# Computing layer 1's memory keys during the routing of layer 0, with own buffers for expert rows

## The chip, the cores and the metric

The kernel runs on one core of a Trainium2 chip. TensorE (PE) multiplies matrices, VectorE (DVE), ScalarE (ACT) and GpSimd (POOL) do the rest, and SyncE (SP) issues most transfers (DMAs) between HBM and the on-chip memory SBUF; matmul results land in banks of PSUM. Each engine works through its own list of instructions in order and waits on semaphores for the others. The metric is the time of one execution on the device, in microseconds (us).

## What the kernel computes

A trunk of two layers on 256 tokens of width 1024, float32. Each layer adds three things to the running state h: a token mixer (layer 0: a recurrent and a sparse-attention group; layer 1: a short gated convolution), a cross-attention over 256 memory tokens, and a mixture of 16 experts. Only the last two matter here:

```python
def memory_cross_attn(xn, mem, g_mem, wq, wk, wv, wo):
    mn = rms_norm(mem, g_mem)
    q, k, v = heads(xn @ wq), heads(mn @ wk), heads(mn @ wv)     # 4 heads of 256
    p = softmax(q @ k^T * 256 ** -0.5)
    return (p @ v) @ wo

def hier_moe(xn, ...):
    # the best of 4 groups, then the best 2 of its 4 experts, gate weights from both
    for e in range(16):
        h = silu(xn @ w_gate[e]) * (xn @ w_up[e])                # 1024 -> 512
        y = y + gate[:, e:e + 1] * (h @ w_down[e])               # 512 -> 1024

for layer in range(2):
    h = h + mixer(rms_norm(h, norm_mix[layer]))
    h = h + memory_cross_attn(rms_norm(h, norm_xattn[layer]), mem, norm_mem[layer], ...)
    h = h + hier_moe(rms_norm(h, norm_ffn[layer]), ...)
return rms_norm(h, norm_final)
```

`mem` is an input, the same for both layers. The keys and values of layer 1 depend on it, on `norm_mem[1]` and on weights, and on nothing that layer 0 computes.

## The kernel before

**Matmuls.** A float32 product is made of three matmuls over a high and a low part: hi·hi, hi·lo, lo·hi. Weights come in tiles w of 1 MB (pool wpool, six buffers), and each 128x1024 piece is split into hi (ACT, L274) and lo (DVE, L275) in the pool spl (three buffers of each). Projections that give the transposed result go into a bank named FA (`proj_F`, L316, L319, L321: 128x256), the others into TA (`proj_T`, L295 to L297: 128x512). `norm_T` normalises, transposes on PE (nB, nC) and splits the result into two tiles such as m1h and m1l, of the pool act8 (four buffers b8).

**Memory keys and values.** `gen_kv(l)` (L357) is a generator of nine steps: the norm of the memory, four steps of keys (FA, into KT), four of values (TA, into VM). For layer 1 one step runs in the odd mixer, four in front of the cross-attention's queries and four between queries and scores. A scheduler of the tile framework orders the instructions of each engine; `with first()` raises the priority of what is inside, so that routing, the softmax and the first gather are pulled forward and the matmuls around them fill the gaps.

**Cross-attention** (L385). Four units of scores sB (L408), softmax on DVE and ACT (L417 to L428), transposes tC and copies to PT (L434, L435), then oB and oC (L443) and the output projection.

**Experts** (`moe`, L775). Routing makes from h: xs, h in two float16 parts (L796 to L805); posm, the place of each token in its experts' 64 seats; vals, the gates with the token numbers. Then come eight pairs of experts. `dispatch` (L554) makes the mask Pm (L561, DVE), gathers the pair's tokens with Pm and xs into banks gB (L578), and copies them with the gain into XgT (L586 ACT, L588 DVE); ptC (L597) fetches gates and row numbers. `expert_pair` (L699) runs gate and up (egA, euA, L712), the activation hs (L722 to L724), its transpose hC and hT (L729, L731), and the down product (eyA, eyO, L736). Six of a layer's pairs scale the result to rows y and scatter them to DRAM (yd<-y, L742 to L745); `add_rows` fetches them back before the last pair (yr<-yd) and adds them to h (L831); the last two pairs go back through poB (L759, L760). Pm, PG, hs, hT, y, yh and yl share the three buffers of the tag s2.

**Weights of the experts.** `Stream` (L664) loads 98 chunks per layer, 1 MB each but for a few of 0.5, in order through SP's queue into a ring of 21 slots, made of free buffers of several pools; a chunk's load is issued when the one that held its slot is used up. Where the number of chunks leaves a rest, the last ones go to the last slots of the ring.

**The overflow branch.** A group with more than 64 tokens for an expert needs extra rounds: `overflow()` reads a count into a register and branches (L812 to L821). With this input it isn't taken. It stands at BREAK = 4, between the fourth and the fifth pair; instructions can't be moved across it.

```python
if n == BREAK:
    run(cur)
    overflow()
    cur = next(pairs)
    run(cur, 3)
    continue
```

Of the kernel before, what the change touches and what calls it, by code (L numbers as in the profile page):

```python
# [9 lines left out]
F32 = mybir.dt.float32  # L10
# [18 lines left out]
NX = 7  # L29
# [30 lines left out]
def hybrid_trunk_kernel(ctx: ExitStack, tc: tile.TileContext, x, mem, positions, norm_mix, norm_xattn,  # L60
# [142 lines left out]
    def sumsq(src, engs="SV"):  # L203
        ss = sm.tile([128, 2, TT], F32, name="ss")
        for tt in range(TT):
            for half in range(2):
                square_sum(src[:, tt, half * 512:(half + 1) * 512], ss[:, half, tt:tt + 1], engs[half])
        return ss
# [26 lines left out]
    def norm_T(src, ss, g, name, xs, tags="BC"):  # L235

        rs = rstd_of(ss)
        V.tensor_scalar(xs[0], src[:, 0, :], rs[:, 0:1], None, op0=ALU.mult)
        S.activation(xs[1], src[:, 1, :], AF.Copy, scale=rs[:, 1:2])
# [13 lines left out]
        return hi, lo  # L253
# [103 lines left out]
    def gen_kv(l):  # L357

        m = kvp.tile([128, 2048], F32, tag="VM", name=f"mem{l}").rearrange("p (t d) -> p t d", t=TT)
        for tt in range(TT):  # L360
            nc.sync.dma_start(m[:, tt, :], mem[0, tt * 128:(tt + 1) * 128, :])
        mh, ml = norm_T(m, sumsq(m, "SS" if l else "SV"), gains["mem", l], f"m{l}", halves(m), tags="BC" if l else "A")
        yield
        KT = kvp.tile([128, J, T], F32, tag="KT", name="KT")
        for half in range(2):
            def use(i, b):
                S.copy(KT[:, half * 4 + 2 * i:half * 4 + 2 * i + 2, :], b)
            yield from gen_F(xa_wk[l], half * 512, 512, mh, ml, use)
        VM = kvp.tile([128, TT, D], F32, tag="VM", name="VM")
        kv_tiles[l] = KT, VM  # L370
        for half in range(2):
            def use(tt, b):
                S.copy(VM[:, tt, half * 512:(half + 1) * 512], b)
            yield from gen_T(col_loads(xa_wv[l], half * 512), mh, ml, use)

# [9 lines left out]
    def cross_attn(l, kv, n_before, n_mid):  # L385
# [9 lines left out]
        KT, VM = kv_tiles[l]  # L395
        Pt = x8([128, TT, 4, T], "Pt")
# [157 lines left out]
    def dispatch(mp, l, xs, gate, vals, posm, e0, n, by_rows):  # L554
# [12 lines left out]
        Xg = [mp.tile([128, J, 128], F32, name="XgT", tag="XgT", bufs=2) for _ in range(n // 2)]  # L567
# [24 lines left out]
        def rest():  # L592
            for pi in range(n // 2):
                if by_rows:
# [9 lines left out]
                    gsl = sm.tile([128, 1], F32, name="gslr", bufs=3)  # L604
                    V.tensor_reduce(gsl, v2[:, 0, 0:3], axis=AX.X, op=ALU.add)
                    row = sm.tile([128, 1], I32, name="row", bufs=3)
# [77 lines left out]
    class Direct:  # L684
# [5 lines left out]
        def take(self, n):  # L690
            t = self.pool.tile([128, n, 1, 512], F32, tag="XgT", name="wov", bufs=2)
            for i in range(n):
                G.dma_start(t[:, i], next(self.chunks)[1])
            return [[t[:, i, 0, :]] for i in range(n)]
# [4 lines left out]
    def expert_pair(mp, l, stream, pair, step, cuts, by_rows, ss=None, rest=None):  # L699
# [39 lines left out]
        def back_by_rows(nh):  # L739
            y = mp.tile([128, 512], F32, name="y", tag="s2", bufs=3)  # L740
# [34 lines left out]
    def moe(l, ring, fill=None, n_fill=0):  # L775
        with ExitStack() as mctx:
            mp = mctx.enter_context(tc.tile_pool(name=f"moe{l}", bufs=1, reuse_waits="tile"))
            if fill is not None:
                run(fill, n_fill)
            stream = Stream(chunks_ahead(l), ring)  # L780
            with first():
# [9 lines left out]

                xsb = act8.tile([128, 2, TT, D], F16, tag="b8", name="xs")
# [437 lines left out]
    def odd_mixer(kv, n_before):  # L1230
# [8 lines left out]
        for half in range(2):  # L1239
# [44 lines left out]
    odd_mixer(kv1, 1)  # L1284
    cross_attn(1, kv1, 4, 4)
    moe(1, ring)
# [41 lines left out]
```

## Time and profile before

| | |
|---|---|
| three runs | 993.76 us median (991.2 to 995.42) |
| the profiled execution | 989.36 us, of which the span is 987.6 |
| even mixer of layer 0 | 0 to about 193 us |
| cross-attention 0, first FA of the queries to the last TA | 193 to 266 |
| routing 0, to the first egA | 266 to 280 |
| experts 0 | 280 to 510 |
| odd mixer, cross-attention 1 | 510 to 722 |
| routing 1, experts 1 | 722 to 978 |
| busy: PE, DVE, ACT, POOL | 91%, 40%, 33%, 9% of the span |
| mean granted clock of PE | 0.96 of full speed |
| moved by DMA | 285.43 MB, mean 289 GB/s |

How to read it: a row of the list in time order has the start and the length in us, the engine, the line of the program, the operation with its tiles (out<-in) and shapes, how many of the kind follow each other, and in brackets how long the engine had been idle before, and what ended that. A matmul's length holds its whole way through the array; matmuls that follow each other overlap, so the distance of two starts is what one costs.

### The profile page before, as it was taken

To read this page: it belongs to the slowest core of one execution; us is meant where nothing else is said; L and a number is where in the kernel's file an instruction comes from. 1 tells how busy PE (TensorE), PEld (TensorE's weight loads), DVE (VectorE), ACT (ScalarE), POOL (GpSimd) and SP (SyncE) were. 2 spreads that over 40 slices of the span, in tenths; PEclk is the share of its full clock that TensorE was granted. 3 is DMA by queue.
4 is the path that set the end of the run, shared out by engine and by line. 5 is a ranking of instruction groups with operands and counts; after the bars stand their busy time and mean duration, and the time that the engine had idled before them with its cause. 6 is when DMAs were issued, how large, how long until landed. Compare 5 with 4: busy or idle time off the path is not lost.

```text
span 987.6 us, 13265 instructions
## 1 busy us (share of the span) xinstructions
PE 898.5 (91%) x5197; PEld 588.7 (60%) x5197; DVE 394.2 (40%) x830; ACT 326.2 (33%) x605; POOL 85.5 (9%) x144
## 2 busy tenths in 40 slices
PE   7999999999989995995989999999989997779795
PEld 5897588898754432332339998998855332323231
DVE  6857686635431111111337665535441111111142
ACT  5655574645411110110146445535421111111112
POOL 1000160000020000012000000000020001000201
PEclk9999899999999997998999999999999999798898
DMA  8955166577879999999875556578869999997861
GB/s 258 307 180 94 43 214 189 178 263 288 343 297 424 418 420 413 421 419 416 308 253 172 171 174 200 155 282 322 317 214 383 418 420 420 415 421 313 331 247 42
DMA packets 83022, 285.43 MB, mean 289 GB/s; under 512 B 15112, under 2 KB 16224, under 8 KB 62468
## 3 DMA queue, kind: packets, MB, share of 16 engines
q1 hardware_dynamic: 78468, 272.82, 73.3%
q0 software_dynamic: 4480, 11.65, 3.4%
q8 instruction: 44, 0.72, 0.3%
q14 instruction: 30, 0.25, 0.1%
HBM read 275.94 MB, written 11.53 MB: 291 GB/s over the span
## 4 chain that ended last, share of the span: by engine, by line
PE 35%; issue 12%; DMA 6%; DVE 2%; ACT 1%; POOL 1%; ACTq 0%; POOLq 0%; DVEq 0%
DMA yd<-y,row 6%; PE egA L712 4%; PE FA L316 4%; PE FA L319 4%; PE FA L321 4%; PE euA L712 3%; PE TA L295 2%; PE TA L296 2%; PE TA L297 2%; PE eyO L736 2%; PE eyA L736 2%; PE gB L578 2%; PE sB L408 1%; PE poB L760 0%; PE hC L729 0%
## 5 line engine op out<-in xcount | busy, mean ns | idle before, releaser
L275 DVE TENSOR_TENSOR lo<-w,hi 128x1024 fp32r<-128x1024 f32 x122 | 147.7, 1222 | 122.9 <-ACT hi L274 83.1
L274 ACT CAST hi<-w 128x1024 fp32r<-128x1024 f32 x122 | 125.9, 1047 | 86.4 <-PE FA L321 47.9
L712 PE MATMUL egA<-we,XgT 128*64 128x512 f32 x512 | 123.2, 613 | 9.9 <-issue 9.9
L712 PE MATMUL euA<-we,XgT 128*64 128x512 f32 x512 | 124.3, 600 | 0.0
L712 PEld LDWEIGHTS euA<-we,XgT 128*64 128x64 f32 x512 | 41.8, 139 | 68.9 <-issue 64.1
L712 PEld LDWEIGHTS egA<-we,XgT 128*64 128x64 f32 x512 | 38.0, 141 | 72.0 <-issue 63.8
L586 ACT ACTIVATE XgT<-gB,ffn 128x128 f32<-128x128 f32 x64 | 22.6, 367 | 175.8 <-DVE XgT L588 175.8
L578 PE MATMUL gB<-Pm,xs 128*128 128x128 f16 x512 | 41.9, 248 | 41.2 <-DVE Pm L561 41.2
L736 PE MATMUL eyA<-we,hT 128*64 128x512 f32 x256 | 73.8, 594 | 2.9 <-ACT hT L731 2.9
L736 PE MATMUL eyO<-we,hT 128*64 128x512 f32 x256 | 76.2, 593 | 0.0
L319 PE MATMUL FA<-xh,hi 128*128 128x256 f32 x272 | 71.0, 294 | 1.8 <-ACT xh L250 1.7
L578 PEld LDWEIGHTS <-xs 128*128 128x128 f16 x512 | 40.2, 151 | 54.4 <-issue 54.3
L321 PE MATMUL FA<-xl,hi 128*128 128x256 f32 x272 | 70.5, 292 | 1.8 <-DVE xl L251 1.8
L742 DVE TENSOR_SCALAR y<-eyO,gslr 128x512 f32<-128x512 f32 x12 | 9.0, 750 | 153.3 <-PE eyO L736 153.3
L319 PEld LDWEIGHTS FA<-xh,hi 128*128 128x128 f32 x272 | 53.6, 197 | 4.8 <-ACT xh L250 2.4
L321 PEld LDWEIGHTS FA<-xl,hi 128*128 128x128 f32 x272 | 53.8, 198 | 3.3 <-DVE xl L251 2.7
L745 POOL DMA_INDIRECT yd<-y,row x24 | 23.8, 991 | 283.5 <-ACT y L744 265.9
L744 ACT ACTIVATE y<-eyA,gslr 128x512 f32<-128x512 f32 x12 | 8.2, 687 | 109.4 <-PE eyA L736 97.2
L736 PEld LDWEIGHTS eyA<-we,hT 128*64 128x64 f32 x256 | 21.3, 137 | 37.8 <-issue 33.0
L736 PEld LDWEIGHTS eyO<-we,hT 128*64 128x64 f32 x256 | 21.9, 137 | 36.7 <-issue 35.0
L316 PE MATMUL FA<-xh,lo 128*128 128x256 f32 x272 | 41.7, 285 | 0.0
L229 POOL TENSOR_TENSOR rs<-ms,mhalf 128x2 f32<-128x2 f32 x9 | 6.5, 720 | 373.7 <-DVE ms L227 252.4
(419 smaller groups left out, 1546.4 us busy)
## 6 DMA issues: line engine op xcount, KB each, us to landing
we<-in_moe_w_gate_dram SPq DMA_DIRECT2D x56, 1024.0 KB, 14.2
we<-in_moe_w_up_dram SPq DMA_DIRECT2D x56, 1024.0 KB, 15.0
we<-in_moe_w_down_dram SPq DMA_DIRECT2D x52, 1024.0 KB, 13.1
w<-in_odd_w_in_dram SPq DMA_DIRECT2D x12, 1024.0 KB, 5.3
w<-in_even_w_in_dram SPq DMA_DIRECT2D x9, 1024.0 KB, 8.8
we<-in_moe_w_down_dram SPq DMA_DIRECT2D x18, 512.0 KB, 16.4
w<-in_xa_wk_dram SPq DMA_DIRECT2D x8, 1024.0 KB, 5.7
w<-in_xa_wv_dram SPq DMA_DIRECT2D x8, 1024.0 KB, 5.7
```

Source lines behind the costliest of these rows:

```text
L274: S.copy(hi, t)
L275: V.tensor_sub(lo, t, hi.bitcast(F32))
L295: P.matmul(ps[tt], xh[:, k, sl], hi, start=(k == 0), stop=False)
L296: P.matmul(ps[tt], xh[:, k, sl], lo, start=False, stop=False)
L316: P.matmul(o, lo[:, fs], xh[:, k, :], start=False, stop=(k == J - 1), skip_group_check=True)
L319: P.matmul(o, hi[:, fs], xh[:, k, :], start=(k == 0 and f % 2 == 0), stop=False, skip_group_check=True)
L321: P.matmul(o, hi[:, fs], xl[:, k, :], start=False, stop=False, skip_group_check=True)
L578: P.matmul(ps[:, jj, :], part[:, tt, :, j0 + jj], Pm[:, tt].rearrange("p e s -> p (e s)"), start=(i == 0), stop=(i == 3))
L586: S.activation(Xg[pi][:, j, :], src, AF.Copy, scale=g)
L712: P.matmul(acc[nm][i * 64:(i + 1) * 64, :], XgT[:, j, i * 64:(i + 1) * 64], ws[i][jj], start=(j == 0), stop=(j == J - 1))
L736: P.matmul(py[nh][i * 64:(i + 1) * 64, :], hT[:, j, i * 64:(i + 1) * 64], w, start=(j == 0), stop=(j == 3))
L745: G.indirect_dma_start(out=Yd[l][nh], out_offset=bass.IndirectOffsetOnAxis(ap=PT[:, 0:1], axis=0), in_=y, in_offset=None, bounds_check=2 * ...
```

## The change

Four edits. (1) The keys of layer 1 become a generator of their own, `gen_keys`: its first step, the norm of the memory, runs in the cross-attention of layer 0 after the values, with the memory in split buffers hi and lo; its four steps of keys run at the start of `moe(0)`. Layer 1 normalises the memory again and computes only values, in two steps before and two between. KT is occupied during layer 0's experts, and the pool extra has six buffers for seven (NX), so the ring has 19 slots in layer 0 and 20 in layer 1. (2) The rows y get a tag of their own with two buffers; the overflow's loads use it too, and its dispatch has its own XgT, gsl and row. (3) The dispatch of the fifth pair is called before the fourth runs on and the branch comes. (4) xs is allocated before `Stream`.

```diff
-NX = 7
+NX = 6
...
-    def gen_kv(l):
-
-        m = kvp.tile([128, 2048], F32, tag="VM", name=f"mem{l}").rearrange("p (t d) -> p t d", t=TT)
+    def mem_T(l, m):
         for tt in range(TT):
-            nc.sync.dma_start(m[:, tt, :], mem[0, tt * 128:(tt + 1) * 128, :])
-        mh, ml = norm_T(m, sumsq(m, "SS" if l else "SV"), gains["mem", l], f"m{l}", halves(m), tags="BC" if l else "A")
-        yield
+            nc.sync.dma_start(m[tt], mem[0, tt * 128:(tt + 1) * 128, :])
+        return norm_T(m, sumsq(m, "SS" if l else "SV"), gains["mem", l], f"m{l}", m, tags="BC" if l else "A")
...
+    def gen_keys(l):
+
+        mh, ml = mem_T(l, [spl.tile([128, D], F32, name="mem1", tag=t) for t in ("hi", "lo")])
+        yield
+        yield from keys(l, mh, ml)
+
+    def gen_values(l):
+
+        mh, ml = mem_T(l, in_VM(l))
+        yield
+        yield from values(l, mh, ml)
...
         run(kv, n_mid)
         KT, VM = kv_tiles[l]
+        if ahead is not None:
+            run(ahead, 1)
...
         def back_by_rows(nh):
-            y = mp.tile([128, 512], F32, name="y", tag="s2", bufs=3)
+            y = mp.tile([128, 512], F32, name="y", bufs=2)
...
             if fill is not None:
                 run(fill, n_fill)
+
+            xsb = act8.tile([128, 2, TT, D], F16, tag="b8", name="xs")
             stream = Stream(chunks_ahead(l), ring)
...
-                            pairs, last_part = dispatch(mp, l, xs, gate, vals, posm2, e, 2, True)
+                            pairs, last_part = dispatch(mp, l, xs, gate, vals, posm2, e, 2, True, "XgO")
...
                 if n == BREAK:
+                    nxt = next(pairs)
                     run(cur)
                     overflow()
-                    cur = next(pairs)
+                    cur = nxt
                     run(cur, 3)
...
-    cross_attn(0, kv0, 2, 2)
+    load_gain("mem", norm_mem, 1)
+    keys1 = gen_keys(1)
+    cross_attn(0, kv0, 2, 2, keys1)
     x, b = [[(extra, "x")]], [[(act8, "b8")]]
-    ring = (x * (NX - 3) + b + [[(kvp, "KT")]] + x * 2 + [[(kvp, "VM")]] + x + b * 2 + [[(wpool, "w")]] * 6
-            + [[(spl, "hi"), (spl, "lo")]] * 3)
-    moe(0, ring)
-    load_gain("mem", norm_mem, 1)
-    kv1 = gen_kv(1)
+
+    def ring(kt):
+        return (x * (NX - 3) + b + kt + x * 2 + [[(kvp, "VM")]] + x + b * 2 + [[(wpool, "w")]] * 6
+                + [[(spl, "hi"), (spl, "lo")]] * 3)
+    moe(0, ring([]), keys1, 4)
+    values1 = gen_values(1)
...
-    odd_mixer(kv1, 1)
-    cross_attn(1, kv1, 4, 4)
-    moe(1, ring)
+    odd_mixer(values1, 1)
+    cross_attn(1, values1, 2, 2)
+    moe(1, ring([[(kvp, "KT")]]))
```

How the edits move PE's instructions, at three places. First the softmax of cross-attention 0. Before, scores sB stand between value matmuls (TA, operands m0h and m0l) and, earlier, between query matmuls (FA):

```order
L295 MATMUL TA<-hi,m0h 128x512
L296 MATMUL TA<-lo,m0h 128x512
L297 MATMUL TA<-hi,m0l 128x512
L408 MATMUL sB<-KT,qT 128x256 x4
L434 MATMUL tC<-ident,Pt 128x128 x8
L295 MATMUL TA<-hi,m0h 128x512
```

Now the end of the 48 value matmuls and of the 16 transposes of the normed memory (nB, nC) stands in front of all scores, with transposes tC and outputs oB and oC behind them:

```order
L249 MATMUL nC<-ident,mem_2316 128x128
L249 MATMUL nC<-ident,mem_2317 128x128
L436 MATMUL sB<-KT,qT 128x256 x12
L462 MATMUL tC<-ident,Pt 128x128 x4
L436 MATMUL sB<-KT,qT 128x256 x4
L462 MATMUL tC<-ident,Pt 128x128 x8
L471 MATMUL oB<-PT,VM 128x256 x4
L462 MATMUL tC<-ident,Pt 128x128 x4
L471 MATMUL oC<-PT,VM 128x256 x4
```

No matmul of another kind is left between the scores and the outputs.

Second, the end of routing 0 on PE. Before, the first gather follows the counts cntC at once:

```order
L504 MATMUL cntC<-selb,ones_b 128x16
L505 LDWEIGHTS ones_b
L505 MATMUL cntC<-selb,ones_b 128x16
L578 LDWEIGHTS xs
L578 MATMUL gB<-Pm,xs 128x128
```

Now 22 key matmuls follow the counts, then ptC (the row numbers of the first pair), then 151 more; the gather comes behind the last of them:

```order
L321 MATMUL FA<-m1h,hi 128x256
L323 MATMUL FA<-m1l,hi 128x256
L318 MATMUL FA<-m1h,lo 128x256 x8
L606 LDWEIGHTS xs
L606 MATMUL gB<-Pm,xs 128x128
```

The other 19 key matmuls stand in front of the counts. xs is written into the buffer that held m1h.

Third, the branch in layer 0. Before, PE's last matmuls in front of it are the downs of the fourth pair, and the fifth pair's gather comes behind it:

```order
L736 MATMUL eyO<-we,hT 64x512
L736 MATMUL eyA<-we,hT 64x512 x2
L736 MATMUL eyO<-we,hT 64x512 x2
L812 TENSOR_LOAD over
L813 COMPARE_AND_BRANCH
```

Now the gather and ptC of the fifth pair stand in front of the fourth pair's last up matmuls:

```order
L606 LDWEIGHTS xs
L606 MATMUL gB<-Pm,xs 128x128
L625 LDWEIGHTS Pm
L625 MATMUL ptC<-vals,Pm 128x10
L625 LDWEIGHTS Pm
L625 MATMUL ptC<-vals,Pm 128x10
L742 MATMUL euA<-we,XgT 64x512 x7
L759 MATMUL hC<-ident,hs 128x128 x4
L766 MATMUL eyA<-we,hT 64x512
```

What was the first work behind the branch is thus done in front of it, and the branch is followed by gate matmuls.

## Rows read from the trace of the kernel before

**Rows 1.** Busy us of an engine, share of the span, instructions; the page's part 1.
```profile
PE 898.5 (91%) x5197; PEld 588.7 (60%) x5197; DVE 394.2 (40%) x830; ACT 326.2 (33%) x605; POOL 85.5 (9%) x144
```

**Rows 2.** The list of waits of PE: total us, times, longest.
```profile
PE gB L578 <- DVE Pm L561: 41.2, 12, 11.5
```

**Rows 3.** PE in order of time, layer 0: start, length, work, [idle before].
```profile
344.02 2.18 PE L578 MATMUL gB<-Pm,xs 128*128 128x128 f16 x32 [0.50 <-DVE Pm L561]
...
387.86 3.57 PE L578 MATMUL gB<-Pm,xs 128*128 128x128 f16 x32 [10.61 <-DVE Pm L561]
...
468.76 1.98 PE L712 MATMUL egA<-we,XgT 128*64 128x512 f32 x4 [9.94 <-issue]
...
509.28 0.73 PE L760 MATMUL poB<-yl,PT 128*128 128x512 f32 x2
```

**Rows 4.** PE in order of time, the experts of layer 1.
```profile
736.92 1.66 PE L712 MATMUL egA<-we,XgT 128*64 128x512 f32 x4
...
845.89 3.57 PE L578 MATMUL gB<-Pm,xs 128*128 128x128 f16 x32 [11.48 <-DVE Pm L561]
...
890.18 2.93 PE L578 MATMUL gB<-Pm,xs 128*128 128x128 f16 x26 [7.28 <-DVE Pm L561]
...
925.65 2.93 PE L578 MATMUL gB<-Pm,xs 128*128 128x128 f16 x26 [7.04 <-DVE Pm L561]
...
977.61 0.73 PE L760 MATMUL poB<-yl,PT 128*128 128x512 f32 x2
```

**Rows 5.** The page's GB/s line; one stretch (busy by engine, PEclk, DMA, GB/s).
```profile
GB/s 258 307 180 94 43 214 189 178 263 288 343 297 424 418 420 413 421 419 416 308 253 172 171 174 200 155 282 322 317 214 383 418 420 420 415 421 313 331 247 42
...
385.00:390.00 5.00, 2.15 (x21) 2.14 (x21) 0.74 (x3) 0.00 (x0) 0.00 (x0) 0.50 1.01 409
```

**Rows 6.** The list of waits of DVE; landing time of the scatter.
```profile
DVE Pm L561 <- DMA yd<-y,row: 63.6, 10, 10.3
...
DVE h L831 <- DMA yr<-yd: 15.6, 3, 11.0
...
DMA to landing us min/median/max: 6.5/7.1/8.1
```

**Rows 7.** PE groups in 612 to 722: count, busy us, mean ns, idle before.
```profile
L319 PE MATMUL FA<-m1h,hi 128*128 128x256 f32 x64 | 15.9, 283 | 0.0
```

**Rows 8.** PE in order of time, cross-attention of layer 0.
```profile
192.67 0.39 PE L297 MATMUL TA<-hi,m0l 128*128 128x512 f32 x1
...
192.90 0.28 PE L319 MATMUL FA<-xah,hi 128*128 128x256 f32 x1
...
193.13 0.28 PE L319 MATMUL FA<-xah,hi 128*128 128x256 f32 x1
...
236.80 1.89 PE L443 MATMUL oB<-PT,VM 128*128 128x256 f32 x8
```

**Rows 9.** DMA issues (KB, us to landing); then DVE and ACT in order of time.
```profile
mem<-in_mem_dram SPq DMA_DIRECT2D x4, 512.0 KB, 7.6
...
207.95 0.69 DVE L417 TENSOR_REDUCE xmx<-sB 128x2 f32<-128x512 f32 x1
...
213.02 0.58 ACT L435 COPY PT<-tC 128x512 f32<-128x512 f32 x1
```

**Rows 10.** PE, POOL in order of time, one stretch: the routing of layer 0.
```profile
265.85 0.39 PE L297 MATMUL TA<-hi,ol 128*128 128x512 f32 x1
...
278.60 1.71 PE L578 MATMUL gB<-Pm,xs 128*128 128x128 f16 x25 [1.09 <-DVE Pm L561]
...
280.27 1.94 PE L712 MATMUL egA<-we,XgT 128*64 128x512 f32 x8
...
271.95 1.25 POOL L805 TENSOR_TENSOR xs<-xt,xs 128x512 f16<-128x512 f32 x1 [2.07 <-ACT xt L804]
...
282.03 0.29 POOL L543 TENSOR_TENSOR vals<-left,vals 128x32 bf16<-128x32 f32 x1
...
266.00:280.00 14.00, 10.62 (x82) 8.12 (x81) 9.78 (x32) 4.80 (x9) 5.38 (x13) 1.00 0.90 337
```

More of the change, by code (lines that the diff above doesn't have):

```diff
@@ L204, in sumsq @@
         ss = sm.tile([128, 2, TT], F32, name="ss")
+        src = src if isinstance(src, list) else halves(src)
         for tt in range(TT):
             for half in range(2):
-                square_sum(src[:, tt, half * 512:(half + 1) * 512], ss[:, half, tt:tt + 1], engs[half])
+                square_sum(src[tt][:, half * 512:(half + 1) * 512], ss[:, half, tt:tt + 1], engs[half])
         return ss
@@ L237, in norm_T @@
         rs = rstd_of(ss)
-        V.tensor_scalar(xs[0], src[:, 0, :], rs[:, 0:1], None, op0=ALU.mult)
-        S.activation(xs[1], src[:, 1, :], AF.Copy, scale=rs[:, 1:2])
+        src = src if isinstance(src, list) else halves(src)
+        V.tensor_scalar(xs[0], src[0], rs[:, 0:1], None, op0=ALU.mult)
+        S.activation(xs[1], src[1], AF.Copy, scale=rs[:, 1:2])
         hi = b8(name + "h", F32R).rearrange("p (j t) -> p j t", j=J)
@@ L355, in hybrid_trunk_kernel, with in_VM, keys @@
     kv_tiles = {}
-    def gen_kv(l):
-        m = kvp.tile([128, 2048], F32, tag="VM", name=f"mem{l}").rearrange("p (t d) -> p t d", t=TT)
+    def mem_T(l, m):
         for tt in range(TT):
-            nc.sync.dma_start(m[:, tt, :], mem[0, tt * 128:(tt + 1) * 128, :])
-        mh, ml = norm_T(m, sumsq(m, "SS" if l else "SV"), gains["mem", l], f"m{l}", halves(m), tags="BC" if l else "A")
-        yield
+            nc.sync.dma_start(m[tt], mem[0, tt * 128:(tt + 1) * 128, :])
+        return norm_T(m, sumsq(m, "SS" if l else "SV"), gains["mem", l], f"m{l}", m, tags="BC" if l else "A")
+    def in_VM(l):
+        return halves(kvp.tile([128, 2048], F32, tag="VM", name=f"mem{l}").rearrange("p (t d) -> p t d", t=TT))
+    def keys(l, mh, ml):
         KT = kvp.tile([128, J, T], F32, tag="KT", name="KT")
+        kv_tiles[l] = [KT]
         for half in range(2):
@@ L374, in gen_kv @@
             yield from gen_T(col_loads(xa_wv[l], half * 512), mh, ml, use)
+    def gen_kv(l):
+        mh, ml = mem_T(l, in_VM(l))
[5 more added lines that the diff above has]
+        yield
+        yield from keys(l, mh, ml)
+    def gen_values(l):
+        mh, ml = mem_T(l, in_VM(l))
+        yield
+        yield from values(l, mh, ml)
     def out_proj(loads_of, xh, xl):
@@ L382, in out_proj, with cross_attn @@
             run(gen_T(loads_of(half), xh, xl, use))
-    def cross_attn(l, kv, n_before, n_mid):
+    def cross_attn(l, kv, n_before, n_mid, ahead=None):
         run(kv, n_before)
@@ L552, in route, with dispatch @@
         return gate, vals, posm, over
-    def dispatch(mp, l, xs, gate, vals, posm, e0, n, by_rows):
+    def dispatch(mp, l, xs, gate, vals, posm, e0, n, by_rows, x_tag="XgT"):
         Pm = mp.tile([128, TT, n, CAP], F16, name="Pm", tag="s2", bufs=3)
@@ L566, in dispatch @@
         N = n * CAP
-        Xg = [mp.tile([128, J, 128], F32, name="XgT", tag="XgT", bufs=2) for _ in range(n // 2)]
+        Xg = [mp.tile([128, J, 128], F32, name="XgT", tag=x_tag, bufs=2 if x_tag == "XgT" else 1) for _ in range(n // 2)]
         per = 512 // N
@@ L603, in rest @@
                     V.tensor_add(v2[:, 0, :], v2[:, 0, :], v2[:, 1, :])
-                    gsl = sm.tile([128, 1], F32, name="gslr", bufs=3)
+                    gsl = sm.tile([128, 1], F32, name="gslr", tag="gsl" + x_tag, bufs=3)
                     V.tensor_reduce(gsl, v2[:, 0, 0:3], axis=AX.X, op=ALU.add)
-                    row = sm.tile([128, 1], I32, name="row", bufs=3)
+                    row = sm.tile([128, 1], I32, name="row", tag="row" + x_tag, bufs=3)
                     V.scalar_tensor_tensor(v2[:, 1, 0:1], v2[:, 0, 4:5], 128.0, v2[:, 0, 3:4], op0=ALU.mult, op1=ALU.add)
@@ L690, in take @@
         def take(self, n):
[L691 to L694, printed above, removed]
+            out = []
+            for _ in range(n):
+                t = self.pool.tile([128, 1, 512], F32, tag="y", name="wov", bufs=2)
+                G.dma_start(t, next(self.chunks)[1])
+                out.append([t[:, 0, :]])
+            return out
         def used(self, n):
@@ L790, in moe @@
                     (S.copy if jp2 % 2 else V.tensor_copy)(hT[jp2 // 2][:, jp2 % 2 * 2:jp2 % 2 * 2 + 2, :], ps)
-                xsb = act8.tile([128, 2, TT, D], F16, tag="b8", name="xs")
                 xsh, xsl = xsb[:, 0], xsb[:, 1]
```

3 lines of the change are left out of this document (2 added, 1 removed).

## The prediction

> **What bounds the kernel now.** I read the page's first table before anything else: TensorE (PE) is busy 91% of the span [rows 1], so a gain has to be matmul time taken away, or PE's waiting. The list of who waited for whom says where PE stands still: 41.2 us in 12 pieces ahead of the gather gB, for the mask Pm that VectorE (DVE) makes [rows 2]. PE's order in time places the long pieces, all among the experts: 10.61 us before 387.86 and another, of 9.94 ahead of egA, before 468.76 in layer 0 [rows 3]; 11.48, 7.28 and 7.04 before 845.89, 890.18 and 925.65 in layer 1 [rows 4]. Third, the GB/s line of the 40 slices (24.7 us each): while the experts run the weights arrive at 413 to 424 in slices 13 to 19 (296 to 469) and 415 to 421 in slices 32 to 36 (766 to 889), and from slice 37 on at 313 and 331 [rows 5]. So the experts of layer 0 stand against two limits that lie close together, the queue nearly to the end; those of layer 1 have slack there, and PE's stalls decide.
>
> **Why PE stalls there.** Pm shares the three buffers of tag s2 with the rows y that are scattered to DRAM. DVE's waits before Pm end on the DMA yd<-y,row (63.6 us in 10), which lands a median 7.1 us after its issue [rows 6]. In a regular pair that is hidden: gB at 344.02 waits 0.50 us [rows 3]. Ahead of the branch it isn't: PE ends at 377.2, then the row is written, scattered and landed before Pm, so that gB starts at 387.86. The 9.94 at 468.76 is another thing: DVE adds the returned rows (h<-h,yr, up to 11.0 us of waiting for yr<-yd [rows 6]) in front of the XgT copies that egA needs.
>
> **The changes, part by part.** All on the profiled execution, 989.4 us (span 987.6); the median of the runs is 993.8, 4.4 more, which I add at the end.
>
> (1) Layer 1 before its experts. The 192 matmuls with m1 as memory and FA as sum go (64 in each of three forms) [rows 7]. Two such steps lie between 192.90 and 193.13 [rows 8], 0.12 us each: 23.0 us. They had no idle time before them [rows 7], and their weight splits go with them, so PE gives all of it back: -23, bounds -18 (some covered a norm or a softmax) and -24. The norm of the memory, with its 16 transposes, stays in layer 1.
>
> (2) Cross-attention of layer 0. Before, its query and value matmuls are strewn between the scores and transposes of the softmax and cover it. Now 192 FA and 48 TA matmuls all run first, then 16 transposes of the normed memory, and only then the scores. 192 x 0.12 + 48 x 0.23 (TA's spacing, 192.67 to 192.90) after 192.90 end at 227 [rows 8]. The memory is loaded into split buffers that come free only when the first value split is used up (about 221); a load of mem takes 7.6 us [rows 9], and sums, root and scaling 4 (in routing the like chain takes 5.7, from 266.2 to 271.95, with an addition and a cast in it [rows 10]): the transposes run at about 233, the scores at 236. Then four softmax units with nothing beside them. The first took 5.65 from its maximum at 207.95 to its copied transpose at 213.60 [rows 9], with two casts in between; four that overlap, about 10. oB starts near 246, where it started at 236.80 [rows 8]: +10, and +2 for PE's clock, which after a wait of 10 us was at 1.2 GHz for 5 us [rows 5]. Bounds +5 (a quicker load, units that overlap better) and +16.
>
> (3) Routing of layer 0. Before, from the last TA (265.85, ends 266.2) to the first egA (280.27) are 14 us, of which PE is idle only 3.4 (busy 10.62 of 14.00), and vals, which the first ptC needs, are ready at 282.3 [rows 10]. Now 41 of the 192 key matmuls go in front of ptC and 151 behind it, and the gather behind all of them. ptC waits for vals, 16.1 us after TA ends; 151 x 0.12 = 18.1; then xs may be written, since its buffer held m1h: ACT once and POOL twice 1.25 [rows 10], 4.0 with hand-over; the gather 1.7 (278.60 to 280.27, from its first to egA). In all 41 against 14: +27. With (2), egA starts at about 319. Bounds: +20 (23.0 less the 3.4 idle) and +33 (vals late, because DVE and ACT first make the splits of the key weights).
>
> (4) Experts of layer 0, 280.27 to 510.0, 229.7 us [rows 3, 10]. Pm no longer waits for y, the dispatch of the pair behind the branch comes before it, and the rows are added behind XgT: 10.6 + 9.9 go, and about 4 us of slow clock behind them (0.50 of full speed in 385 to 390, 2.5 us, and the recovery [rows 5]). PE alone would need 205. But now the queue decides. The 98 chunks make 96 of 1.049 MB; 19 slots are full when egA starts, 77 follow, with 5.2 MB of rows (12 scattered and 8 fetched, of 128x512 in fp32): 86 MB at 420 GB/s are 205 us. Before, 75 chunks by the same sum take 200; with the first refill some 5 us after egA the last byte lands at 486, and the rate falls in slice 20 (469 to 494) [rows 5], which agrees. So the last byte lands 210 us after egA, and behind it come the last pair's downs. 98 leaves a rest of 3 by 19 slots, so the last three chunks wait for slots used three chunks earlier, and I add 10: 220, that is -10. Bounds 211 (a tail of 1 us) and 228.
>
> The Trainium skill ("DMA: Bandwidth & Descriptors", Specifications) gives about 358 GB/s as what HBM can hand one core. By 358 the two expert stages would take some 255 and 248 us, both longer than now, and the change would lose about 45. The GB/s line shows 413 to 424 for 170 us on end, so the row decides.
>
> (5) Experts of layer 1, 736.92 to 978.3, 241.4 us. The stalls 11.5+7.3+7.0 = 25.8 go [rows 4], and about 5 us of slow clock behind them, by (4): PE needs 211. The queue with 20 slots: 76 chunks and the rows, 202 + 5 + 5 = 212. I take 215: -26. Bounds 211 and 224.
>
> (6) At nothing: the second norm's DVE and ACT work in layer 1 (it was there before); the two y buffers (a pair writes two rows every 25 us, 205 over eight pairs, against 7.1 for the landing [rows 6]); the longer filling of the ring before egA (the queue has 37 us more for it).
>
> Sum: -23 + 12 + 27 - 10 - 26 = -20: 969 in the profile, **974** by the runs' median.
>
> **Rivals.** A, slower: the weights. With the stalls gone both expert stages hang on the queue, 205 + 202 us, on fewer slots and in order. Break-even is 407 x (420/b - 1) = 20, b = 400 GB/s; at 383, the rate of slice 31, when the ring of layer 1 has just begun to drain [rows 5], +39, so 1013. For it: every wait of PE now reaches the queue at once through 19 slots. Against: 413 and more under the same scatters.
> B, the cover holds: the keys fill routing (+20) and the softmax costs +5, -14 more: 960. For it: part of PE's time in routing is filler matmuls. Against: xs waits for the last key in any case.
> C, the experts of layer 1 keep half of their stalls, since y, hs or the stream take over from Pm: -13 instead of -26, and 987. For it: two buffers for y where s2 had three. Against: the spacing in (6).
> D, the 358 of the page under the new load: +45, 1040; rows 5 speak against it.
>
> **How the numbers follow.** Forecast 0.62 (own range 962 to 984), A 0.09, B 0.13, C 0.15, D 0.01. About 0.5% (5 us) is what a measurement of this kernel can tell from no change: faster is below 988.8, slower above 998.7. Faster: the forecast 0.62, B 0.13, a third of C 0.05, 0.80; same: the rest of C and a little of A, 0.12; slower: the rest of A and D, 0.08. The range 953 to 991 leaves out A, D and the far ends of (1) to (5).
>
> **What would show it.** Right: m1's FA matmuls between 250 and 320 and none in layer 1; egA's first start at 315 to 323; no wait of gB above 2 us; 410 GB/s and more throughout the experts of layer 0, which end near 540, those of layer 1 near 958 in the profile. Wrong: egA at 305 (B) or past 330; a stage of 230 again in layer 0 with egA waiting for we (A); gB or eyA still waiting for y or Pm (C). It falls as a whole if the gather of layer 0 runs before the keys are done, or if no stall goes.

## The result, and the profile after

The changed kernel takes 998.77 us in the median of 17 runs (991.0 to 1004.8), the kernel before 990.17 beside it: a ratio of 1.0067, 95% interval 1.0041 to 1.0093. It is slower, by 0.7%; 974 was forecast. The profiled execution has a span of 996.0 us, 8.4 more than before. One profile of an experiment below (banks A) is of an execution 9 us longer than that kernel's median; only its cross-attention of layer 0 is read, up to the start of the output.

PE is busy for 922.6 us where it was for 898.5 [rows 1]; it isn't waiting that made the kernel longer, since the idle rest fell from 89 to 73. The matmuls that were added are the 16 transposes of the second norm.

```profile
PE 922.6 (93%) x5213; PEld 595.8 (60%) x5213; DVE 399.8 (40%) x841; ACT 332.9 (33%) x622; POOL 87.5 (9%) x145
```

The long waits for Pm are gone (41.2 us in 12 [rows 2] became 1.1), but the list of PE's waits has new names in their place (us in total, times, longest): poB, which waits for yl; the branch, seen from DVE (DVEq is its sequencer); and the second norm of the memory.

```profile
PE poB L790 <- DVE yl L785: 8.3, 2, 4.5
...
PE egA L742 <- DVEq L843: 6.4, 1, 6.4
...
PE nB L249 <- DVE mem L240: 5.8, 1, 5.8
...
PE gB L606 <- DVE Pm L589: 1.1, 1, 1.1
```

The table sets the stages of the two kernels side by side. Each end is a row's start (egA's first, the last TA) or the end of the last poB; of before they are in [rows 3, 4, 8, 10], the first FA of the queries at 192.90, the first TA of the output at 243.51, the last TA of layer 1 at 721.56.

| stage | before | after | measured | forecast |
|---|---|---|---|---|
| cross-attention 0: queries to output | 50.6 | 64.1 | +13.4 (+1.9 of a later start) | +12 |
| routing 0: last TA to first egA | 14.4 | 42.1 | +27.7 | +27 |
| experts 0: first egA to last poB | 229.7 | 233.3 | +3.5 | -10 |
| layer 1 in front of its routing | 211.6 | 188.5 | -23.0 | -23 |
| routing 1 | 15.4 | 14.5 | -0.9 | 0 |
| experts 1 | 241.4 | 226.9 | -14.5 | -26 |

PE in cross-attention 0, in order of time (start, length, work, [idle before]):

```profile
228.53 0.39 PE L299 MATMUL TA<-hi,m0l 128*128 128x512 f32 x1
...
234.70 1.29 PE L249 MATMUL nB<-ident,mem 128*128 128x128 f32 x4 [5.78 <-DVE mem L240]
...
238.42 3.85 PE L436 MATMUL sB<-KT,qT 128*128 128x256 f32 x16
...
251.62 1.99 PE L471 MATMUL oB<-PT,VM 128*128 128x256 f32 x8 [0.73 <-ACT PT L463]
```

TA of the values ends near 229, the transposes of the memory start 5.78 us later, and all scores stand behind them; oB starts at 251.62 against 236.80 [rows 8]. Routing 0:

```profile
281.26 0.39 PE L299 MATMUL TA<-hi,ol 128*128 128x512 f32 x1
...
298.27 0.19 PE L625 MATMUL ptC<-vals,Pm 128*128 128x10 bf16 x2 [3.17 <-POOL vals L571]
...
317.52 0.34 PE L606 MATMUL gB<-Pm,xs 128*128 128x128 f16 x2 [0.85 <-DVE xs L826]
...
318.84 0.35 PE L606 MATMUL gB<-Pm,xs 128*128 128x128 f16 x2 [0.97 <-DVE xs L830]
...
320.97 2.46 PE L606 MATMUL gB<-Pm,xs 128*128 128x128 f16 x21 [1.78 <-POOL xs L835]
...
323.36 0.98 PE L742 MATMUL egA<-we,XgT 128*64 128x512 f32 x2
```

ptC waits 3.17 us for vals, the keys run from there to 316.7, and the gather waits three times, 3.6 us together, for xs, which is written only then. The first egA starts at 323.36 against 280.27 [rows 10]. The experts of layer 0, against [rows 3]:

```profile
421.80 1.08 PE L766 MATMUL eyO<-we,hT 128*64 128x512 f32 x4
...
429.31 3.68 PE L742 MATMUL egA<-we,XgT 128*64 128x512 f32 x8 [6.44 <-DVEq L843]
...
528.63 1.03 PE L790 MATMUL poB<-yl,PT 128*128 128x512 f32 x2 [4.48 <-DVE yl L785]
...
548.93 1.07 PE L766 MATMUL eyO<-we,hT 128*64 128x512 f32 x2 [0.77 <-DMA we<-in_moe_w_down_dram]
...
555.90 0.73 PE L790 MATMUL poB<-yl,PT 128*128 128x512 f32 x2
```

10.61 us in front of the fifth pair became 6.44, for DVE's branch; the 9.94 became 4.48 in another place, in front of poB; and the last down chunk comes late. The experts of layer 1, against [rows 4]:

```profile
859.04 4.49 PE L742 MATMUL egA<-we,XgT 128*64 128x512 f32 x12 [2.39 <-DMA we<-in_moe_w_gate_dram]
...
864.71 1.88 PE L742 MATMUL egA<-we,XgT 128*64 128x512 f32 x7 [1.18 <-issue]
...
959.56 1.22 PE L790 MATMUL poB<-yl,PT 128*128 128x512 f32 x2 [3.83 <-DVE yl L785]
...
985.82 0.73 PE L790 MATMUL poB<-yl,PT 128*128 128x512 f32 x2
```

Of 25.8 us, 2.39, 1.18 and 3.83 are left. But the waits are only a part of it. Here are the two expert stages by busy time, layer 0 and then layer 1, first of the kernel before (stretch, length, busy of PE, PEld, DVE, ACT and POOL, granted clock, DMA share, GB/s):

```profile
280.27:510.01 229.74, 202.81 (x1064) 82.55 (x1063) 44.11 (x114) 29.61 (x66) 20.07 (x33) 0.95 0.97 391
736.92:978.34 241.42, 209.20 (x1064) 84.90 (x1063) 44.52 (x114) 29.61 (x66) 21.15 (x30) 0.94 0.85 344
```

and then of the changed kernel:

```profile
323.36:556.63 233.27, 214.28 (x1062) 82.46 (x1061) 44.65 (x109) 29.53 (x66) 18.47 (x27) 0.97 0.94 378
759.61:986.55 226.94, 212.21 (x1064) 84.40 (x1063) 45.37 (x114) 29.64 (x66) 21.85 (x32) 0.97 0.91 371
```

PE's idle time fell by 7.9 us in layer 0 (26.9 to 19.0) and by 17.5 in layer 1 (32.2 to 14.7). Its busy time for the same matmuls grew, by 11.5 and by 3.0, at a mean granted clock that is no lower (0.97 in both, where it was 0.95 and 0.94). (Two matmuls ptC of layer 0 stand in front of the first egA now.) The page's GB/s line [rows 5]:

```profile
GB/s 257 305 177 93 43 211 184 179 188 254 223 227 225 345 419 419 417 416 418 420 413 153 356 180 206 166 173 240 299 314 276 421 418 420 414 421 418 416 339 42
```

The queue gave 413 to 420 in slices 15 to 21 and 414 to 421 in 32 to 38 (slices of 24.9 us), as before. But for the last down chunks of layer 0 and 2.39 us behind the branch of layer 1, PE waits for no weights. The rate of 358 GB/s that the Trainium skill gives (DMA: Bandwidth & Descriptors, Specifications) bounds nothing here either.

### The profile page after: what moved, and what is told of

It is laid out like the page before. It is cut to its first block, busy times and chain, and to the rows that moved or that the text cites. A ratio compares the mean times of both kernels' runs of the same rounds, so it can differ in the third digit from the quotient of the medians.

```text
span 996.0 us, 13307 instructions
## 1 busy us (share of the span) xinstructions
PE 922.6 (93%) x5213; PEld 595.8 (60%) x5213; DVE 399.8 (40%) x841; ACT 332.9 (33%) x622; POOL 87.5 (9%) x145
## 4 chain that ended last, share of the span: by engine, by line
PE 30%; DMA 18%; issue 4%; DVE 2%; POOL 1%; ACT 1%; ACTq 0%; POOLq 0%; SPq 0%; DVEq 0%
DMA we<-in_moe_w_gate_dram 5%; DMA we<-in_moe_w_up_dram 4%; DMA we<-in_moe_w_down_dram 4%; PE egA L742 4%; PE euA L742 4%; DMA yr<-yd 3%; PE FA L318 3%; PE FA L323 3%; PE FA L321 3%; PE TA L297 2%; PE TA L298 2%; PE TA L299 2%; PE eyO L766 2%; PE eyA L766 2%; PE gB L606 1%
## 5 line engine op out<-in xcount | busy, mean ns | idle before, releaser
L742 PE MATMUL euA<-we,XgT 128*64 128x512 f32 x512 | 126.5, 615 | 0.0
L606 PEld LDWEIGHTS <-xs 128*128 128x128 f16 x512 | 34.7, 148 | 24.6 <-issue 20.6
L754 DVE SCALAR_TENSOR_TENSOR hs<-hs,euA 128x512 f32<-128x512 f32 x16 | 11.0, 687 | 95.5 <-PE euA L742 95.5
L606 PE MATMUL gB<-Pm,xs 128*128 128x128 f16 x512 | 38.5, 231 | 4.7 <-POOL xs L835 1.8
L753 DVE SCALAR_TENSOR_TENSOR hs<-hs,egA 128x512 f32<-128x512 f32 x16 | 11.0, 686 | 78.1 <-ACT hs L752 78.1
L318 PE MATMUL FA<-xh,lo 128*128 128x256 f32 x272 | 41.7, 284 | 0.0
L616 DVE TENSOR_SCALAR XgT<-gB,ffn 128x128 f32<-128x128 f32 x64 | 21.5, 349 | 46.1 <-PE gB L606 36.0
## 6 DMA issues: line engine op xcount, KB each, us to landing
w<-in_odd_w_in_dram SPq DMA_DIRECT2D x12, 1024.0 KB, 14.5
```

Source lines behind the costliest of these rows:

```text
L318: P.matmul(o, lo[:, fs], xh[:, k, :], start=False, stop=(k == J - 1), skip_group_check=True)
L606: P.matmul(ps[:, jj, :], part[:, tt, :, j0 + jj], Pm[:, tt].rearrange("p e s -> p (e s)"), start=(i == 0), stop=(i == 3))
L616: V.tensor_scalar(Xg[pi][:, j, :], src, g, None, op0=ALU.mult)
L742: P.matmul(acc[nm][i * 64:(i + 1) * 64, :], XgT[:, j, i * 64:(i + 1) * 64], ws[i][jj], start=(j == 0), stop=(j == J - 1))
```

## The experiments

There are twelve kernels, in three groups, each in three rounds or more beside the kernel before; a ratio is to the runs of before in the same group. "Experts" means first egA to the last poB's end, from each kernel's own trace.

| kernel | median | ratio to before (95%) | experts 0 | experts 1 |
|---|---|---|---|---|
| before | 990 | 1 | 229.7 | 241.4 |
| changed | 998.77 | 1.0067 (1.0041 to 1.0093) | 233.3 | 226.9 |
| keys only | 1005.81 | 1.0184 (1.0130 to 1.0238) | 241.3 | 229.5 |
| no keys | 972.13 | 0.9824 (0.9781 to 0.9867) | 226.2 | 227.4 |
| banks A | 991.42 | 1.0003 (0.9973 to 1.0033) | | |
| no branch | 988.25 | 0.9985 (0.9953 to 1.0018) | 228.7 | 224.0 |
| 18 slots | 1007.94 | 1.0159 (1.0113 to 1.0204) | 242.3 | 227.6 |
| dispatch only | 986.85 | 0.9964 (0.9935 to 0.9994) | 236.7 | 231.4 |
| y only | 973.66 | 0.9810 (0.9744 to 0.9876) | 227.4 | 227.3 |
| rows late | 960.30 | 0.9686 (0.9627 to 0.9745) | 223.2 | 219.6 |
| no keys, 19 slots | 980.02 | 0.9902 (0.9869 to 0.9935) | 233.8 | 227.3 |
| keys at their best | 973.03 | 0.9836 (0.9796 to 0.9876) | 225.4 | 220.5 |
| before, rows late | 976.57 | 0.9875 (0.9837 to 0.9913) | 217.9 | 240.9 |
| y, rows late | 955.61 | 0.9663 (0.9625 to 0.9702) | 220.3 | 216.8 |

**Keys only.** From the changed kernel, with the lines of before elsewhere:

```diff
-NX = 6
+NX = 7
...
-            y = mp.tile([128, 512], F32, name="y", bufs=2)
+            y = mp.tile([128, 512], F32, name="y", tag="s2", bufs=3)
...
-                    nxt = next(pairs)
                     run(cur)
                     overflow()
-                    cur = nxt
+                    cur = next(pairs)
```

> Only edit 1: layer 1's keys in the routing of layer 0, memory normed twice; rows y in tag s2 as before, dispatch behind the branch as before, 20 ring slots in layer 0 and 21 in layer 1. Theory (by the stages of the changed kernel's trace): the scores of cross-attention 0 start late, +15; routing grows by 28; layer 1 in front of its experts loses 23; experts as before: +20, about 1010 us. Rival (the keys pay for themselves and the loss comes from fewer slots and the other edits): within 5 us of before.

Slower by 1.8%, some 17 us: the keys don't pay for themselves. The stages in front of the experts came as expected (routing 42.1, layer 1's front 188.5). The experts did not stay as before: layer 0 is 11.5 longer and layer 1 12.0 shorter. The waits of 7 us for Pm moved from layer 1 to layer 0, and the wait of 10 us in front of egA from layer 0 to layer 1 (10.9). Which layer has which is thus not a property of the layer; it goes with the order in which the instructions are laid out.

**No keys.** The other half: all edits but the keys.

```diff
-    cross_attn(0, kv0, 2, 2, keys1)
+    cross_attn(0, kv0, 2, 2)
...
-    moe(0, ring([]), keys1, 4)
-    values1 = gen_values(1)
+    moe(0, ring([[(kvp, "KT")]]))
+    load_gain("mem", norm_mem, 1)
+    kv1 = gen_kv(1)
```

> The changed kernel with edit 1 undone: all keys in layer 1, memory normed once for it, 20 ring slots in both layers; y buffers, dispatch in front of the branch and xs ahead of the ring stay. Theory (PE's own waits set the experts' time, the queue doesn't): experts 0 about 230 to 233, experts 1 about 227, the rest as before: 977 to 982. Rival (19 slots and the late last three chunks cost layer 0 its gain): experts 0 fall to 220, total about 966.

972.13, 1.8% faster than before. It fell below the theory's range and short of the rival's: experts 0 at 226.2, 7.1 less than in the changed kernel, which the theory did not have. Within the change the keys cost some 26 us.

**Banks A.**

```diff
-    def mem_T(l, m):
+    def mem_T(l, m, tags=None):
...
-        return norm_T(m, sumsq(m, "SS" if l else "SV"), gains["mem", l], f"m{l}", m, tags="BC" if l else "A")
+        return norm_T(m, sumsq(m, "SS" if l else "SV"), gains["mem", l], f"m{l}", m, tags=tags or ("BC" if l else "A"))
...
-        mh, ml = mem_T(l, [spl.tile([128, D], F32, name="mem1", tag=t) for t in ("hi", "lo")])
+        mh, ml = mem_T(l, [spl.tile([128, D], F32, name="mem1", tag=t) for t in ("hi", "lo")], "A")
```

> The changed kernel, but the transposes of the second memory norm in cross-attention 0 use the PSUM banks A in place of B and C. Theory (the scores wait for banks B that the memory's transposes were given first): the scores go back among the query and value matmuls, oB starts near 237 and the total falls by 12 to 15, to about 985. Rival (the load and norm of the memory hold up the softmax by their work on ACT and DVE): at most 4 us less, 995 or more.

PE in order of time, the first query matmul and the first oB:

```profile
199.25 0.28 PE L321 MATMUL FA<-xah,hi 128*128 128x256 f32 x1
...
243.16 1.02 PE L471 MATMUL oB<-PT,VM 128*128 128x256 f32 x4
```

oB comes 43.9 us behind the queries' start, as before (236.80 - 192.90 = 43.9), so the theory on the scores holds: the softmax had lost its cover because the transposes of the memory were handed banks B and C ahead of the scores, not by their work. The output starts 54.5 behind the queries, 9.6 earlier than in the changed kernel and 3.8 later than before: the 16 transposes now stand around the last oC, in front of the output. The total fell by 6 to 7 (each against its own runs of before), half of what was expected; the 3.8 had been left out.

**No branch.** The overflow branch is left out, and the fourth pair runs into the fifth as other pairs do:

```diff
-BREAK = 4
+BREAK = 99
```

> The changed kernel without the overflow branch (left out; it isn't taken with this input), so that no pair is cut off from the next. Theory (PE's waits at the branch are its own cost: 6.4 us for VectorE in layer 0, 2.4 and 1.2 in layer 1, and slow clock behind them): 12 to 15 us less, about 985. Rival (the weights' queue is the limit in the experts, so that a wait removed comes back as a wait for we): 4 us or less, 995.

Experts 0 are 4.6 shorter, experts 1 2.9, the total by some 9. The wait of 6.44 is gone, and nothing waits for we in its place but 1.7 us of one down chunk; neither side had the size right.

**18 slots.**

```diff
-    moe(0, ring([]), keys1, 4)
+    moe(0, ring([])[1:], keys1, 4)
```

> The changed kernel with 18 ring slots in layer 0 in place of 19 (98 chunks then leave a rest of 8, so the last chunks wait for slots used 8 chunks earlier, not 3). Theory (19 slots cost layer 0 only by the rest of 3, which holds back its last down chunks): the waits of eyO for we at the end go, experts 0 get 2 to 4 us shorter. Rival (fewer slots starve the stream): experts 0 get longer by 2 us or more.

Slower by 9, and no clean test of the question: no wait for the last down chunks is left, as the theory has it, but the instructions were laid out anew, and DVE now adds the fetched rows in front of an expert's hs, so that PE waits 14.8 us for it:

```profile
PE hC L759 <- DVE hs L754: 18.0, 5, 14.8
```

**Dispatch only** and **y only**, both against the kernel without keys. First the dispatch only:

```diff
-            y = mp.tile([128, 512], F32, name="y", bufs=2)
+            y = mp.tile([128, 512], F32, name="y", tag="s2", bufs=3)
```

> Keys in layer 1, dispatch of the fifth pair in front of the branch, but the rows y share tag s2 with Pm as before; 20 slots. Theory (the two edits remove different waits: the dispatch the wait at the branch down to the branch's own 6.3 and 2.4 us, the y buffers those of 7 us in pairs 6 and 7): 5 to 8 us slower than with both, 978 to 981. Rival (the dispatch alone does it, y is never in its way then): 972, as with both.

Then the y buffers only:

```diff
-                    nxt = next(pairs)
                     run(cur)
                     overflow()
-                    cur = nxt
+                    cur = next(pairs)
```

> Keys in layer 1, rows y in two buffers of their own, but the fifth pair's dispatch behind the branch as before; 20 slots. Theory: at the branch PE waits for it (6.3 in layer 0, 2.4 in layer 1) and then for Pm, gather and XgT, some 4 us more in each layer than with both edits; the waits of 7 us go: about 980. Rival (the branch was all of the wait in layer 0): 972 to 974.

The buffers do nearly all of it: with y alone 973.66, with the dispatch alone 986.85, which is 6 us more than the theory gave and 3 less than before. PE's waits for Pm (total us, times, longest), first with the dispatch alone:

```profile
PE gB L606 <- DVE Pm L589: 34.6, 13, 7.7
```

and then with y alone:

```profile
PE gB L606 <- DVE Pm L589: 7.4, 4, 2.8
```

With the rows in s2 the waits of 7 us come back in both layers. With y out of the way but the dispatch behind the branch, the longest wait for Pm is 2.8 us. The expected 980 for y alone was wrong: it counted the branch's 6.3 as a cost there too, and it isn't (below).

**Rows late.** No keys, and the fetched rows are added one step later:

```diff
+            yrs = []
+
             def add_rows():
...
+                    yrs.append(yr)
+
+            def add_fetched():
+                for yr in yrs:
                     for tt in range(TT):
                         V.tensor_add(h[:, tt, :], h[:, tt, :], yr[:, tt, :])
...
                 run(cur)
+                if n == NE // 2 - 1:
+                    add_fetched()
                 run(nxt, 1)
```

> Keys in layer 1, all other edits, and the returned rows yr are added to h behind the seventh pair's own results, not in front of them on VectorE. Theory (poB waits for yl, which stands behind the additions: 2.0 and 5.3 us, and some slow clock behind them): 6 to 9 us less than 972, about 965. Rival (the additions then end later than the last pair and hold up the end of the layer): 972 or more.

960.30, 11.8 less than without the edit, more than the theory gave. By stages it is 3.1 us in experts 0 and 7.8 in experts 1. The wait of poB for yl is gone from the list.

**No keys, 19 slots.** Against the kernel without keys:

```diff
-    moe(0, ring([[(kvp, "KT")]]))
+    moe(0, ring([]))
```

> Keys in layer 1 and all other edits, but layer 0's ring without the KT slot: 19 slots, as in the changed kernel. Theory (of the 7 us that experts 0 lose with the keys, most come from the 19 slots: the last three chunks wait for slots used three chunks earlier, and what PE does behind them): experts 0 go from 226 to 231 to 233, total 977 to 979. Rival (the keys' late start is what costs, by the order of the work): 226 and 972.

Experts 0 go from 226.2 to 233.8, the changed kernel's 233.3: in this layout the slot costs what the keys seemed to cost there. The wait for yl, 2.03 with 20 slots, is longer, and PE waits for the last down chunks (below). Its idle time grew by only 2.6 us, though; the other 5.0 are busy time, 215.5 against 210.5.

```profile
487.80 1.22 PE L790 MATMUL poB<-yl,PT 128*128 128x512 f32 x2 [4.43 <-DVE yl L785]
...
508.64 1.07 PE L766 MATMUL eyO<-we,hT 128*64 128x512 f32 x2 [1.00 <-DMA we<-in_moe_w_down_dram]
```

**Keys at their best.** The changed kernel with banks A, as above, and the rows late; of the edit, the call:

```diff
                 run(cur)
+                if n == NE // 2 - 1:
+                    add_fetched()
```

> The changed kernel with the keys in routing 0, with banks A for the second norm and the returned rows added late: everything that was found, with the keys left in. Theory (the keys cost the same matmul time in either layer, and routing of layer 0 has only 3.4 us of idle time to hide them in; the serial chain behind the last key adds the rest): 10 to 18 us slower than the same without the keys (960), 970 to 978. Rival (the keys were slow by the lost softmax cover and the late rows alone): 960 to 965.

12.7 us slower than the same without keys, as the theory had it. By stages: routing +28.0, cross-attention +3.8, experts 0 +2.3, experts 1 +0.9, layer 1's front -23.2, 11.8 together. The experts of layer 0 have 19 slots here as in the changed kernel, and lose 2.3 by them and the keys, not 7.6.

**Before, rows late.** The kernel before with the edit of rows late, and nothing else; of the edit, the call:

```diff
                 run(cur)
+                if n == NE // 2 - 1:
+                    add_fetched()
                 run(nxt, 1)
```

> The kernel before, with one edit: the returned rows yr are added to h behind the seventh pair's own results. Theory (the 9.9 us wait of egA in layer 0 came from the additions in front of the XgT copies; layer 1 had no such wait): 7 to 10 us less in layer 0, nothing in layer 1, about 981. Rival (the wait is for the rows' scatter and Pm, and moves to another place): 987 to 992.

976.57, 1.25% faster from one moved call. Experts 0 are 11.9 shorter, where the theory had 7 to 10, and experts 1 as before (240.9), as the theory says. The last poB of layer 0 starts here, against 509.28 [rows 3]:

```profile
495.92 0.74 PE L760 MATMUL poB<-yl,PT 128*128 128x512 f32 x2
```

**y, rows late.** Rows late, no keys, with the dispatch behind the branch:

```diff
-                    nxt = next(pairs)
                     run(cur)
                     overflow()
-                    cur = nxt
+                    cur = next(pairs)
```

> Keys in layer 1, own y buffers, returned rows added late, but the fifth pair's dispatch behind the branch. Theory (with y out of the way the dispatch in front only trades a wait for Pm, the gather and XgT against the wait for the branch itself): within 4 us of 960. Rival (the dispatch in front is worth a wait of its own): 966 or more.

955.61, the fastest of all, 3.4% faster than before and 43 us faster than the changed kernel. It is just below the theory's 956 to 964. The dispatch in front of the branch costs about 3 us in each layer (223.2 against 220.3, 219.6 against 216.8). What it avoided was 2.6 us of waiting for Pm, and what it met was a wait at the branch, of 6.4 us in layer 0 and 2.4 in layer 1. In layer 1 the two waits are alike, and the difference is busy time of PE (209.7 against 206.2).

## Why the prediction was wrong

**(1) and (3), right.** The keys' 192 matmuls cost 23.0 us in layer 1 and came back as 27.7 in routing 0, with the terms named: vals at 298.3, 17 us behind TA, then 151 matmuls, then xs, then the gather. (The terms written add up to 39.9, not to the 41 put there; 41.7 were measured by that count.) The keys had nothing to hide in. With banks A and the rows late a loss of 12.7 us remains, 3.8 of it by the second norm in the cross-attention and 2.3 in the experts of layer 0.

**(2), right in size, and its cause confirmed in part.** +13.4 and a start 1.9 later for +12. The steps of the chain came in the order written, each some us later, 1.9 of them by the later start: 5.78 us of waiting for the memory, transposes at 234.7 for 233, scores at 238.4 for 236, oB at 251.6 for 246. From the scores to oB it took 13.2 us, where some 10 and 2 for the clock were put; the granted clock was 0.81 of full speed from 243 to 252. What the prediction didn't name is why the scores stand behind the transposes: the two banks B. Given other banks, the scores went back among the matmuls.

**(4), wrong: the queue was said to decide at 220, and PE decided, at 233, by its waits and by a longer busy time.** The step that failed is that the stalls go whole and leave PE 205 us by itself. PE was busy for 214.3 us and idle for 19.0. Of the 20.5 us of waits that were to go, 7.9 went, net of new ones; and the busy time, which was to fall by the slow clock, grew by 11.5. Three readings failed with it, the first two on the waits.

First, "10.6 + 9.9 go" without asking what is late next, though the trace of before held the answer. DVE's sequencer at the branch, in the kernel before (ns; start in layer 0 and in layer 1):

```profile
L813 DVEq COMPARE_BRANCH  x2: 63/68/72, 377.9 to 834.9; - x2
...
L813 DVEq EVENT_SEMAPHORE  x2: 21/21/21, 383.4 to 835.5; - x2
```

It is 5.5 us from the comparison to the next step in layer 0, and Pm had to wait longer than that for the scatter of y, so the 10.61 hid it. In the changed kernel nothing covers it:

```profile
L843 DVEq COMPARE_BRANCH  x2: 63/68/72, 423.5 to 857.1; - x2
...
L843 DVEq EVENT_SEMAPHORE  x2: 21/21/21, 429.2 to 857.7; - x2
```

In layer 0 DVE comes through 5.7 us behind its comparison, in layer 1 0.6 behind, and egA waits for it.

Second, the 9.94 in front of egA did go, but the additions stood in front of yl instead. DVE in order of time:

```profile
516.57 1.23 DVE L861 TENSOR_TENSOR h<-h,yr 128x1024 f32<-128x1024 f32 x1 [7.82 <-DMA yr<-yd]
...
522.13 1.23 DVE L861 TENSOR_TENSOR h<-h,yr 128x1024 f32<-128x1024 f32 x1 [4.34 <-DMA yr<-yd]
...
526.68 1.22 DVE L861 TENSOR_TENSOR h<-h,yr 128x1024 f32<-128x1024 f32 x1 [0.90 <-DMA yr<-yd]
...
527.83 0.74 DVE L785 SCALAR_TENSOR_TENSOR yl<-eyA,gsl,yh 128x512 fp32r<-128x512 f32 x1
```

yl runs 1.15 us behind the last addition's start, and that one waited for the fetch; poB waited 4.48 for yl. The kernel before with the rows late shows the price of these additions in its own layout, where they stood in front of XgT: 11.9 us.

Third, 19 slots. The rest of 3 was seen and priced at a few us, as part of a tail of 10. In the kernel without keys the slot costs 7.6. Issues of SP's queue, first of the changed kernel, then without keys:

```profile
544.27 4.29 SPq L700 DMA_DIRECT2D we<-in_moe_w_down_dram  x6
```

```profile
460.95 21.44 SPq L700 DMA_DIRECT2D we<-in_moe_w_down_dram  x7
```

With 19 slots the last six down pieces are issued only at 544 to 549, with PE already at the last pair's downs (the one at 548.93 waits for its weights); with 20 slots seven of them go out from 461 to 482, 25 us and more ahead of that layer's end at 507.

That late issue is not all of the 7.6. In keys at their best these pieces go out just as late, at 522.6 to 526.8 with the first egA at 309.4; PE waits 0.9 us for them, and the stage is only 2.3 longer than with 20 slots and no keys. So the slot was dear with the additions in front of yl and cheap with the rows late; how the two act on each other, no run shows.

Edit by edit, experts 0 go from 220.3 (y, rows late) by 2.9 (dispatch in front), 3.1 (rows in front of yl) and 7.6 (19 slots) to 233.8 (no keys, 19 slots); the changed kernel has 233.3, so the keys themselves add nothing there. The sizes hold in this order only: from keys at their best to the changed kernel the rows (with the banks) are worth 7.9. That 220.3 is the number that was forecast from the queue is chance: no wait for weights is in its list.

The queue's own figure held for all but the last three chunks: slice 22, from 523 on, has 153 GB/s, some 9 us at the full rate, so that the rate falls near 532, 209 us behind the first egA, where 210 were forecast. The last three chunks, in six pieces, were issued up to 225 us behind it. And the up and down work of the last pair takes PE 25 us behind the fall of the rate, where a tail of 10 was put. The forecast had that figure in hand: 486 for the last byte of before, and 510 for the end.

**(5), wrong in the same term.** "25.8 go" held for the waits named, but idle time fell by 17.5 only, since new waits came, and PE was busy for 3.0 us more. From y, rows late (216.8) the dispatch in front costs 2.8 and the rows in front of yl 7.8, which makes the 227.4 of no keys; the changed kernel has 226.9. Without both edits the 215 of the forecast is nearly reached.

**(6)** held for y: two buffers were enough, and alone they brought 16.5 us against before, as much as all edits without the keys (16.9 in their own runs). The longer filling of the ring did no harm either: PE waits for no weights until the end of that layer.

**The rivals.** A (the weights starve PE) has the right sign for the wrong reason: the rate stayed at 413 and more. B is refuted: nothing of the keys was hidden. C came closest: the experts of layer 1 kept half of their stalls, 14.5 gained of 26, but mainly by yl and the branch, not by y, hs or the stream. The other stages, as measured, sum to -23.0 + 15.3 + 27.7 - 0.9 = +19: the change lived on the stalls of both expert stages being worth 36, and they were worth 11.

**What stays open.** Why the branch takes DVE 5.7 us in some layouts and 0.6 in others (last section). And what makes PE's busy time in the experts longer: 214.3 us in layer 0 of the changed kernel, 209.5 in y, rows late, 202.8 before and 201.3 in before, rows late, for the same matmuls. One part can be read from the starts of PE's rows: the gathers and ptC are strewn more finely, so that PE steps 16 times from an expert's matmul to one of them where it did so 8 times before, at some 0.53 us each, against 0.22 on average for a step from one expert's matmul to the next. By an estimate from these numbers that is 2 to 3 of the 11.5 us. No run isolates the rest.

## What to carry to other kernels

Work that is moved from one stage in which TensorE is the bound to another can gain only the idle time that it fills there, here at most 3.4 us (none of it was gained), and pays for every buffer and bank that it holds: ask for each which instruction was handed it next. Before a stall is written off, list what else waits at that place and how long it would wait alone; the 5.5 us of the branch and the 11.0 for which the additions wait [rows 6] were in the trace of before. Count busy time as well as waits: the same matmuls took PE 11.5 us more in another order. And a wait of 10 us that an engine's order makes (an addition that nobody needs yet, in front of one that PE waits for) can be worth nearly as much as a change of the buffers: one moved call gave 1.25% by itself, the y buffers 1.9%.

## What the runs showed of the hardware

At the overflow branch the engines jump over a body that isn't run. From its comparison to its next step DVE took 5.5 to 5.7 us in layer 0 and 0.6 in layer 1 in ten of the thirteen kernels that have the branch, the one before and the changed one among them. In the other three, dispatch only, y only and y, rows late, it was 0.6 in both layers. Where the dispatch stands doesn't decide it: it is in front of the branch in dispatch only as in the changed kernel, and behind it in y only as in the kernel before. Dispatch only (columns as above):

```profile
L843 DVEq COMPARE_BRANCH  x2: 63/68/72, 382.1 to 846.2; - x2
...
L843 DVEq EVENT_SEMAPHORE  x2: 21/21/21, 382.7 to 846.7; - x2
```

and y, rows late:

```profile
L843 DVEq COMPARE_BRANCH  x2: 63/68/72, 374.4 to 820.6; - x2
...
L843 DVEq EVENT_SEMAPHORE  x2: 21/21/21, 375.0 to 821.1; - x2
```

The Trainium skill (Runtime: NRT & Kernel Launch, Instruction fetch mechanics) says that a jump to a place outside the fetched pages makes the engine wait for its instructions to be loaded. It would explain a cost that depends on how much code lies between the jump and its target and where. No run here varied that alone, and in the 5.9 us from the comparison on the queues of instructions move four packets in the changed kernel (5.7 us) as in y, rows late (0.6 us), so it isn't shown.
